# A list scheduler with refitted durations and an attention rank 100 places ahead, in a three-branch mixer kernel

## Chip, cores and metric

One core of one Trainium2 chip runs the whole program. The metric is the device time of one launch in microseconds (us), the median of several runs. The engines are PE (matrix products, transposes), ACT, DVE and POOL (elementwise work), and SP, whose queue issues the DMAs.

## What is computed

Two layers over 512 latent tokens and a prefix of 256 context tokens, width 1024, all fp32. Cut to what matters:

```python
for l in range(2):
    h  = rms_norm(x, g_pre) * (1 + scale) + shift          # also for the context tokens
    rk, rv, dk, dv, rq, rg, dq, dg, mu, mv, mg, mlog = split(h @ w_in[l])
    # (A) retention, 4 heads, chunks of 128, both directions, rotary q and k
    ret  = rms_norm(bidir_retention(rope(rq), rope(rk), rv)) * silu(rg)
    # (B) gated MLP with 128x128 position mixing
    mlp  = mu * (w_s @ layer_norm(mv) + b_s) * silu(mg)
    # (C) differential attention, 4 heads, keys = context + latent (768)
    p    = softmax(q @ k.T / 8)                             # two maps per head
    dif  = rms_norm((p[0] - lam * p[1]) @ dv) * silu(dg)
    y    = sum(sigmoid(logit_b) * (branch_b @ w_bo[b]) for the three branches)
    x    = x + gate * rms_norm(y @ w_out[l], g_post)
```

In the second layer the context tokens only give keys, values and a final retention state.

## The kernel before

**Products.** A large product is made of three fp32r products of high and low parts (`xs`, `ws`): activations and weights are split into a rounded high part (copied by ACT) and the rest (a subtraction on DVE). Weights come in blocks of 2048 or 1536 words per partition, by one DMA each into one of two raw buffers, and are split into one of two slots (`w_split`, 512 words at a time). A projection takes a tile of PSUM in the first two of eight banks; ACT or DVE empties it (`.ev`), and only then can the tile after next be written.

**Attention unit** (`d_unit`, one head and 128 queries, 32 of them with six key tiles, 8 with two): PE makes the scores of two maps in three banks that all units share; DVE takes the maxima (L370); ACT makes two exponentials with sums (L339); DVE combines them (L378, L360, L366); PE transposes the result (L318); ACT copies it; PE multiplies by the values (L314, fp32, two records per instruction in the profile); then a norm over ACT, DVE and POOL, one transpose and a copy. **Retention unit** (`r_state`, `r_attn`): similar, shorter chains.

**Order of the code.** `dr_phase` walks through the projections of the attention and retention branches in the order of `ORDER`; after each tile `step` lets one or two finished units be recorded (`pop`), so the units lie between projections whose results they don't need. After it come the gates (`dg`), merges, the MLP and the output. Each `add` records one operation with its engine, a cost in ns, what it reads and writes, and a rank: its place in the recording, plus `bump`:

```python
o.prio = o.i + self.bump
```

Weight splits are recorded with a bump of -20 (`WBUMP`), so they rank 20 places ahead.

**Scheduler.** `Rec.schedule` plays the recorded operations against its own costs: an engine that is free takes the lowest rank among the operations that are ready, an operation is ready when all that it depends on have ended plus `LATENCY[from, to]`. What comes out is one fixed order per engine, and the instructions are emitted in it. On the chip each engine works through its own queue in that order and waits on semaphores: an operation that is not ready holds up all behind it, ready or not.

Of the kernel before, what the change touches and what calls it, by code (L numbers as in the profile page):

```python
# [12 lines left out]
ALU = mybir.AluOpType  # L13
AX = mybir.AxisListType
# [172 lines left out]
class Op:  # L187
# [1 line left out]

LATENCY = {("PE", "ACT"): 200, ("PE", "DVE"): 200, ("PE", "SP"): 200, ("ACT", "PE"): 290, ("ACT", "DVE"): 100, ("ACT", "POOL"): 100,
           ("ACT", "SP"): 100, ("ACT", "ACT"): 100, ("DVE", "PE"): 290, ("DVE", "ACT"): 150, ("DVE", "POOL"): 170, ("DVE", "DVE"): 127,
           ("DVE", "SP"): 100, ("POOL", "PE"): 150, ("POOL", "ACT"): 65, ("POOL", "DVE"): 65, ("POOL", "POOL"): 102, ("POOL", "SP"): 100}

WINDOW = 3413.3

# [1 line left out]
class Rec:  # L199
# [123 lines left out]
    def act(self, out, in_, func, bias=None, scale=1.0, accum=None):  # L323
        kw = {}
        ins, outs = [in_], [out]
        if bias is not None:
            kw["bias"] = bias
            if not isinstance(bias, float):
                ins.append(bias)
        if not isinstance(scale, float):  # L330
            ins.append(scale)
        kw["scale"] = scale
        c = self.n(in_) / 1.19 + (160 if self.ps(in_) else 195) + 198 * (accum is not None) + 60 * (len(ins) - 1)
        if accum is not None:
            kw["accum_out"] = accum
            outs.append(accum)
        tab = "e" if func == AF.Exp else "s" if func == AF.Sigmoid else None
        e = self.nc.scalar
        return self.add("ACT", lambda: e.activation(out, in_, func, **kw), outs, ins, c, tab)  # L339
# [3 lines left out]

    def copy_v(self, out, in_):
        v = self.nc.vector
        c = self.n(in_) / (0.96 if self.ps(in_) or self.ps(out) else 1.92) + 160
        return self.add("DVE", lambda: v.tensor_copy(out, in_), [out], [in_], c)

    def tt(self, out, a, b, op):
        v = self.nc.vector  # L350
        return self.add("DVE", lambda: v.tensor_tensor(out, a, b, op=op), [out], [a, b], self.n(out) / 0.97 + 168)  # L351

    def ts(self, out, a, s1, s2=None, op0=ALU.mult, op1=None):
        v = self.nc.vector
        ins = [a] + [s for s in (s1, s2) if s is not None and not isinstance(s, float)]
        c = self.n(out) * (1.04 if self.ps(a) else 0.52) + 160 + 60 * (len(ins) - 1)
        if op1 is None:
            f = lambda: v.tensor_scalar(out, a, s1, None, op0=op0)  # L358
        else:
            f = lambda: v.tensor_scalar(out, a, s1, s2, op0=op0, op1=op1)  # L360
        return self.add("DVE", f, [out], ins, c)

    def stt(self, out, a, s, b, op0, op1):
        v = self.nc.vector
        ins = [a, b] + ([] if isinstance(s, float) else [s])
        return self.add("DVE", lambda: v.scalar_tensor_tensor(out, a, s, b, op0=op0, op1=op1), [out], ins, self.n(out) / 0.97 + 215)  # L366

    def red(self, out, in_, op):
        v = self.nc.vector
        return self.add("DVE", lambda: v.tensor_reduce(out, in_, axis=AX.X, op=op), [out], [in_], self.n(in_) / 0.96 + 155)  # L370

    def ttr(self, junk, a, b, accum):
        v = self.nc.vector
        return self.add("DVE", lambda: v.tensor_tensor_reduce(junk, a, b, 1.0, 0.0, ALU.mult, ALU.add, accum), [junk, accum], [a, b], self.n(a) / 0.96 + 290)  # L374

    def recip(self, out, in_):
        v = self.nc.vector
        return self.add("DVE", lambda: v.reciprocal(out, in_), [out], [in_], self.n(in_) * 6.25 + 155)  # L378

    def bn_stats(self, out, in_):  # L380
        v = self.nc.vector
        return self.add("DVE", lambda: v.bn_stats(out, in_), [out], [in_], self.n(in_) / 0.96 + 155)

    def bn_aggr(self, out, in_):
        v = self.nc.vector
        return self.add("DVE", lambda: v.bn_aggr(out, in_), [out], [in_], 172)

    def ptt(self, out, a, b, op):
        g = self.nc.gpsimd
        n = self.n(out)  # L390
        c = 600 + 150 * n if op == ALU.pow else 2.4 * n + 250
        return self.add("POOL", lambda: g.tensor_tensor(out, a, b, op=op), [out], [a, b], c)  # L392

    def memset(self, out, val):
# [9 lines left out]
    def schedule(self):  # L404
# [23 lines left out]
        while ev:  # L428
# [4 lines left out]
            while again:  # L433
                again = False
                for e in self.ENG:
# [13 lines left out]

                    t0 = max((x + LATENCY[f, e] for b in o.banks for f, x in held[b].items() if (f == "PE") != (e == "PE")), default=0.0)  # L450
                    if t0 > t:
# [26 lines left out]
                    for s in succ[i]:  # L478
                        left[s] -= 1
                        at[s] = max(at[s], o.done + LATENCY.get((e, ops[s].eng), 0))  # L480
                        if left[s] == 0:
# [78 lines left out]
NBUF = 4  # L560
BUMP = 400
WBUMP = -20
H_LO = 6144
RING = (12288, 16384)
Z = 20480
# [5 lines left out]
class Prog:  # L571
    def __init__(self, nc, R, AR, AFl, PSM, ap):
# [4 lines left out]
        self.HH = self.arv(0, 8, NT)  # L577
        self.HL = self.arv(H_LO, 8, NT)
        self.raws = {}
# [61 lines left out]
    def w_split(self, i):  # L641
# [9 lines left out]
        step = 512  # L651
        R.bump = WBUMP
        for a in range(0, w, step):
# [67 lines left out]
    def pop(self):  # L721
        f = (self.side[0] or self.side[1]).pop(0)[1]
        t = self.R.tag
        f()
        self.R.tag = t

    def until(self, key):
# [1137 lines left out]
```

## Time and profile before

| | |
|---|---|
| median of 3 runs | 1536.49 us (1535.66 to 1537.17) |
| the profiled execution | 1536.63 us |
| its span, first to last instruction | 1534.9 us |
| PE busy | 1505.0 us, 98% |
| PE weight loads busy | 1350.8 us, 88% |
| DVE / ACT / POOL busy | 799.0 / 602.3 / 168.9 us |
| TensorE clock granted | 1.00 of full, from the start to the end |
| DMA | 156.32 MB, mean 102 GB/s |

The profiled execution lies 1.7 us above its span and 0.14 us above the median. A row of the timeline merges instructions of one kind that follow each other; the time in square brackets is the idle time of the engine before the row, with the instruction that ended it. The end of a matrix product is modelled and lies after the time at which the next product may start, so of a row of n products the array is taken for less than its length.

### The profile page before, as it was taken

The page shows a single profiled execution, that of the slowest core. Times are in us where ns is not written, and L with a number is a line of the kernel's source. Part 1 is how long each engine was busy: PE and PEld are TensorE (multiplying, and loading weights), DVE is VectorE, ACT ScalarE, POOL GpSimd, SP SyncE. Part 2 cuts the span into 40 slices and gives each one's busy share as a digit, 9 for nine tenths or more (in the row PEclk, how much of TensorE's full clock was granted, in tenths as well). Part 3 has the DMA queues.
Part 4 walks back from the last instruction along what each step waited for, and adds up shares of the span by engine and source line. Part 5 has one row for each costly group of instructions (what it writes and reads, how often), then busy time and mean ns, then how long its engine had stood idle before and what let it go on. Part 6 is the DMA issues. An engine that isn't in the chain of part 4 may idle for free.

```text
span 1534.9 us, 23633 instructions
## 1 busy us (share of the span) xinstructions
PE 1505.0 (98%) x9544; PEld 1350.8 (88%) x9544; DVE 799.0 (52%) x1551; ACT 602.3 (39%) x1298; POOL 168.9 (11%) x187
## 2 busy tenths in 40 slices
PE   7999999999999999999999999999999999999998
PEld 4799998989888888989889999989988888898888
DVE  4457635655333872235874654674656434344452
ACT  6735543573222222222223463464455333332341
POOL 1212201110000011001000131111110000201000
PEclk9999999999999999999999999999999999999999
DMA  9441312111231442122563223241211332321331
GB/s 364 144 138 56 86 40 76 50 52 63 75 116 54 165 138 83 56 74 88 187 201 124 97 101 121 86 117 49 83 42 56 103 117 83 118 98 65 119 124 69
DMA packets 37710, 156.32 MB, mean 102 GB/s; under 512 B 5345, under 2 KB 6497, under 8 KB 31201
## 3 DMA queue, kind: packets, MB, share of 16 engines
q1 hardware_dynamic: 37600, 154.81, 30.0%
q8 instruction: 75, 1.23, 0.3%
q14 instruction: 35, 0.28, 0.1%
HBM read 132.77 MB, written 4.19 MB: 89 GB/s over the span
## 4 chain that ended last, share of the span: by engine, by line
PE 94%; issue 1%; DVE 1%; ACT 1%; DMA 0%; POOL 0%; SPq 0%; DVEq 0%; POOLq 0%; ACTq 0%
PE PSM L314 91%; PE PSM L318 3%; ACT AF L339 1%; DMA AF<-AF 0%; POOL AF L392 0%; DVE AR L351 0%; SPq L401 0%; DVE AF L351 0%; DVE AF L366 0%; DVE AF L370 0%; ACT AR L339 0%; DVE AF L360 0%; DVE AF L378 0%; DVEq L1861 0%; POOLq L1861 0%
## 5 line engine op out<-in xcount | busy, mean ns | idle before, releaser
L314 PE MATMUL PSM<-AR 128*128 128x256 f32 (+1 forms) x8016 | 1361.8, 330 | 9.1 <-ACT AF L339 7.3
L314 PEld LDWEIGHTS PSM<-AR 128*128 128x128 f32 x8016 | 1186.5, 190 | 140.7 <-ACT AF L339 9.6
L339 ACT ACTIVATE AR<-AF 128x512 fp32r<-128x512 f32 (+4 forms) x489 | 285.2, 607 | 422.3 <-PE PSM L314 295.9
L351 DVE TENSOR_TENSOR AR<-AF,AR 128x512 fp32r<-128x512 f32 (+4 forms) x486 | 318.6, 673 | 252.6 <-ACT AR L339 205.2
L339 ACT ACTIVATE AF<-PSM 128x512 f32<-128x512 f32 (+4 forms) x385 | 170.5, 462 | 392.1 <-PE PSM L314 324.3
L392 POOL TENSOR_TENSOR AF<-AF 128x1 f32<-128x1 f32 (+5 forms) x180 | 168.2, 943 | 1360.9 <-DVE AF L360 588.5
L351 DVE TENSOR_TENSOR AF<-PSM,AF 128x512 f32<-128x512 f32 (+2 forms) x253 | 144.7, 581 | 236.6 <-PE PSM L314 111.8
L314 PE MATMUL PSM<-AF 128*128 128x128 f32 (+3 forms) x1104 | 143.9, 304 | 12.4 <-DMA AF<-wmodn 8.9
L314 PEld LDWEIGHTS PSM<-AF 128*128 128x128 f32 (+1 forms) x1104 | 127.2, 184 | 23.9 <-DVE AF L360 9.3
L339 ACT ACTIVATE AF<-PSM,AF 128x768 f32<-128x768 f32 (+2 forms) x144 | 91.9, 648 | 64.9 <-DVE AF L358 40.5
L374 DVE CUSTOM_DVE_ANT_0 AR<-AF 128x1024 fp32r<-128x1024 f32 x59 | 76.5, 1296 | 14.8 <-DMA AF<-wmod 8.8
L370 DVE TENSOR_REDUCE AF<-PSM 128x2 f32<-128x1536 f32 (+1 forms) x40 | 61.4, 1541 | 35.7 <-PE PSM L314 35.6
L360 DVE TENSOR_SCALAR AF<-AF 128x1 f32<-128x1 f32 (+3 forms) x188 | 42.5, 237 | 61.5 <-ACT AF L339 58.3
L318 PE MATMUL PSM<-AF 128*128 128x128 f32 x424 | 67.5, 277 | 2.1 <-DVE AF L366 1.2
L339 ACT ACTIVATE AF<-AF 128x256 f32<-128x256 f32 (+4 forms) x107 | 54.7, 558 | 20.4 <-POOL AF L392 10.3
L318 PEld LDWEIGHTS PSM<-AF 128*128 128x128 f32 x424 | 51.2, 142 | 13.1 <-ACT AF L339 3.2
L351 DVE TENSOR_TENSOR AF<-AF 128x512 f32<-128x512 f32 (+5 forms) x78 | 42.9, 555 | 13.2 <-PE PSM L318 5.0
L366 DVE SCALAR_TENSOR_TENSOR AF<-AF 128x768 f32<-128x768 f32 (+2 forms) x48 | 43.5, 913 | 3.6 <-POOL AF L392 2.7
L366 DVE SCALAR_TENSOR_TENSOR AF<-AF,PSM 128x128 f32<-128x128 f32 x64 | 19.8, 344 | 20.5 <-PE PSM L314 12.0
L358 DVE TENSOR_SCALAR AF<-AF 128x2 f32<-128x2 f32 (+4 forms) x98 | 20.4, 223 | 7.0 <-PE PSM L314 3.4
L360 DVE TENSOR_SCALAR AF<-PSM,AF 128x128 f32<-128x128 f32 x48 | 15.9, 404 | 12.0 <-PE PSM L318 11.9
L351 DVE TENSOR_TENSOR AR<-PSM,AR 64x256 fp32r<-64x256 f32 x24 | 10.1, 421 | 21.2 <-ACT AR L339 21.0
(20 smaller groups left out, 94.3 us busy)
## 6 DMA issues: line engine op xcount, KB each, us to landing
AF<-w SPq DMA_DIRECT2D x50, 1024.0 KB, 4.8
AF<-w SPq DMA_DIRECT2D x48, 768.0 KB, 4.2
AF<-wmod SPq DMA_DIRECT2D x32, 512.0 KB, 3.6
AF<-wmodn SPq DMA_DIRECT2D x16, 512.0 KB, 8.9
AF<-x SPq DMA_DIRECT2D x12, 512.0 KB, 4.2
AR<-AR SPq DMA_DIRECT2D x16, 384.0 KB, 4.6
AF<-AF SPq DMA_DIRECT2D x64, 64.0 KB, 2.3
AR<-AF SPq DMA_DIRECT2D x12, 256.0 KB, 2.3
```

The source lines that it names most:

```text
L314: self.add("PE", lambda: pe.matmul(out, lhsT, rhs, start=start, stop=stop), [out], [lhsT, rhs], c)
L318: self.add("PE", lambda: pe.transpose(out, in_, ident), [out], [in_, ident], 109.0)
L339: return self.add("ACT", lambda: e.activation(out, in_, func, **kw), outs, ins, c, tab)
L351: return self.add("DVE", lambda: v.tensor_tensor(out, a, b, op=op), [out], [a, b], self.n(out) / 0.97 + 168)
L358: f = lambda: v.tensor_scalar(out, a, s1, None, op0=op0)
L360: f = lambda: v.tensor_scalar(out, a, s1, s2, op0=op0, op1=op1)
L366: return self.add("DVE", lambda: v.scalar_tensor_tensor(out, a, s, b, op0=op0, op1=op1), [out], ins, self.n(out) / 0.97 + 215)
L370: return self.add("DVE", lambda: v.tensor_reduce(out, in_, axis=AX.X, op=op), [out], [in_], self.n(in_) / 0.96 + 155)
L374: return self.add("DVE", lambda: v.tensor_tensor_reduce(junk, a, b, 1.0, 0.0, ALU.mult, ALU.add, accum), [junk, accum], [a, b], self.n(a) ...
L392: return self.add("POOL", lambda: g.tensor_tensor(out, a, b, op=op), [out], [a, b], c)
```

## The change

The latencies between engines and the fixed parts of the costs on ACT, DVE and POOL get new numbers, nearly all smaller; costs on PE and of DMAs stay. Whatever `pop` records (attention and retention units, with the code that ends a head) gets a bump of -100. No operation is added or removed, and what depends on what stays: only the orders differ.

```diff
-LATENCY = {... ("ACT", "PE"): 290, ("ACT", "DVE"): 100, ("ACT", "POOL"): 100,
-           ("ACT", "SP"): 100, ("ACT", "ACT"): 100, ("DVE", "PE"): 290, ("DVE", "ACT"): 150, ("DVE", "POOL"): 170, ("DVE", "DVE"): 127,
-           ("DVE", "SP"): 100, ("POOL", "PE"): 150, ("POOL", "ACT"): 65, ("POOL", "DVE"): 65, ...}
+LATENCY = {... ("ACT", "PE"): 153, ("ACT", "DVE"): 133, ("ACT", "POOL"): 177,
+           ("ACT", "SP"): 135, ("ACT", "ACT"): 135, ("DVE", "PE"): 137, ("DVE", "ACT"): 119, ("DVE", "POOL"): 163, ("DVE", "DVE"): 117,
+           ("DVE", "SP"): 117, ("POOL", "PE"): 93, ("POOL", "ACT"): 73, ("POOL", "DVE"): 73, ...}
 # act
-        c = self.n(in_) / 1.19 + (160 if self.ps(in_) else 195) + 198 * (accum is not None) + 60 * (len(ins) - 1)
+        c = self.n(in_) / 1.19 + (60 if self.ps(in_) else 95) + 150 * (accum is not None) + 88 * (len(ins) - 1)
 # tt (copy_v, ts, red, recip, bn_stats, bn_aggr in the same way, some 84 less; stt 85 less, ttr 140 less)
-        return self.add("DVE", lambda: v.tensor_tensor(out, a, b, op=op), [out], [a, b], self.n(out) / 0.97 + 168)
+        return self.add("DVE", lambda: v.tensor_tensor(out, a, b, op=op), [out], [a, b], self.n(out) / 0.97 + 84)
 # ptt
-        c = 600 + 150 * n if op == ALU.pow else 2.4 * n + 250
+        c = 560 + 150 * n if op == ALU.pow else 2.4 * n + 210
...
+ABUMP = -100
...
     def pop(self):
         f = (self.side[0] or self.side[1]).pop(0)[1]
         t = self.R.tag
+        self.R.bump = ABUMP
         f()
+        self.R.bump = 0
         self.R.tag = t
```

The orders themselves, at three places of PE's queue. `PSM<-AR` are fp32r products: in these places x2 of 512 columns and x2 or x4 of 256 are the scores of an attention unit, x24 of 256 is half of a projection's pair of tiles, x12 of 512 half of a tile. `L318` are transposes, `L314 ... PSM<-AF 128x128 x6` the products of one unit with its values.

**Place A**, PE, layer 0, units 1 and 2 of the last attention head. Before (the first, second, fifth and sixth rows are the scores of unit 1; the last two begin those of unit 2):

```order
L314 MATMUL PSM<-AR 128x512 x2
L314 MATMUL PSM<-AR 128x256 x2
L318 MATMUL PSM<-AF 128x128
L314 MATMUL PSM<-AF 128x128 x2
L314 MATMUL PSM<-AR 128x256 x2
L314 MATMUL PSM<-AR 128x512 x2
L318 MATMUL PSM<-AF 128x128 x8
L314 MATMUL PSM<-AR 128x512 x2
L314 MATMUL PSM<-AR 128x256 x2
```

After (scores of unit 1 in the first three rows, scores of unit 2 from the last row on):

```order
L314 MATMUL PSM<-AR 128x512 x2
L314 MATMUL PSM<-AR 128x256 x4
L314 MATMUL PSM<-AR 128x512 x2
L314 MATMUL PSM<-AR 128x256 x24
L318 MATMUL PSM<-AF 128x128
L314 MATMUL PSM<-AF 128x128 x6
L314 MATMUL PSM<-AR 128x256 x24
L318 MATMUL PSM<-AF 128x128 x7
L314 MATMUL PSM<-AR 128x512 x2
```

Between the two units' scores stood eight transposes; now a whole pair of projection tiles, six products and eight transposes stand there.

**Place B**, PE, layer 0, the last query projection of retention (`rq1`, x12 of 512) and the key-value projection after it (`rkv3`, x24 of 256). Before:

```order
L314 MATMUL PSM<-AR 128x512 x16
L314 MATMUL PSM<-AR 128x256 x2
L314 MATMUL PSM<-AR 128x512 x12
L314 MATMUL PSM<-AR 128x256 x24
L314 MATMUL PSM<-AR 128x512 x2
```

After (the first row ends `rq1`; the third is another tile pair of `rkv3`, whose PSUM was emptied long before; the pair that needs the tile of `rq1` is the end of the last row):

```order
L314 MATMUL PSM<-AR 128x512 x14
L314 MATMUL PSM<-AF 128x128 x6
L314 MATMUL PSM<-AR 128x256 x24
L318 MATMUL PSM<-AF 128x128 x7
L314 MATMUL PSM<-AR 128x512 x2
L314 MATMUL PSM<-AR 128x256 x4
L314 MATMUL PSM<-AR 128x512 x2
L314 MATMUL PSM<-AF 128x128 x6
L314 MATMUL PSM<-AR 128x256 x24
L318 MATMUL PSM<-AF 128x128
L314 MATMUL PSM<-AR 128x256 x32
```

The tile that is written next after `rq1` was the one that `rq1` itself had just filled before; now two halves of another pair and two units' work come between.

**Place C**, PE, layer 1, units 0 to 2 of the last attention head. Before (the first two rows end the scores of unit 1, the sixth, seventh, ninth and tenth are those of unit 2, the eleventh transposes unit 1 and the twelfth multiplies it):

```order
L314 MATMUL PSM<-AR 128x256 x2
L314 MATMUL PSM<-AR 128x512 x2
L318 MATMUL PSM<-AF 128x128 x2
L314 MATMUL PSM<-AF 128x128 x6
L318 MATMUL PSM<-AF 128x128 x2
L314 MATMUL PSM<-AR 128x512 x2
L314 MATMUL PSM<-AR 128x256 x2
L318 MATMUL PSM<-AF 128x128
L314 MATMUL PSM<-AR 128x256 x2
L314 MATMUL PSM<-AR 128x512 x2
L318 MATMUL PSM<-AF 128x128 x6
L314 MATMUL PSM<-AF 128x128 x6
```

After (the first row ends the scores of unit 1; the seventh transposes unit 1, the last multiplies it):

```order
L314 MATMUL PSM<-AR 128x512 x2
L318 MATMUL PSM<-AF 128x128 x8
L314 MATMUL PSM<-AR 128x256 x24
L318 MATMUL PSM<-AF 128x128
L314 MATMUL PSM<-AF 128x128 x6
L314 MATMUL PSM<-AR 128x256 x24
L318 MATMUL PSM<-AF 128x128 x7
L314 MATMUL PSM<-AR 128x512 x2
L314 MATMUL PSM<-AR 128x256 x4
L314 MATMUL PSM<-AR 128x512 x2
L314 MATMUL PSM<-AF 128x128 x6
```

Two halves of a projection pair now stand between the scores of unit 1 and its transposes, where before stood only small work of the units themselves, and the next unit's scores stand between the transposes and the product.

Elsewhere: PE's order is the same from the second layer's first merge to the end; from the first layer's first merge to that layer's end only a few neighbours change places. On SP the first 59 DMA issues stand as before, and none of the 318 moves by more than 5 places. On ACT and DVE an operation moves by 2 to 3 places in the mean, at most by some 30.

## Rows read from the trace of the kernel before

**Rows 1.** The page's part 1: PE's busy time, share of the span, instructions.
```profile
PE 1505.0 (98%) x9544; PEld 1350.8 (88%) x9544; DVE 799.0 (52%) x1551; ACT 602.3 (39%) x1298; POOL 168.9 (11%) x187
```

**Rows 2.** Stretches: length, busy time of each engine, clock, DMA share, GB/s.
```profile
8.90:24.00 15.10, 13.01 (x69) 5.94 (x70) 8.05 (x23) 9.82 (x18) 3.94 (x6) 1.00 1.04 405
24.00:62.00 38.00, 38.00 (x252) 28.69 (x253) 20.77 (x84) 27.88 (x72) 0.46 (x1) 1.00 0.62 230
62.00:398.00 336.00, 328.70 (x2268) 303.26 (x2267) 189.49 (x392) 165.39 (x419) 54.35 (x71) 1.00 0.23 72
398.00:913.00 515.00, 515.00 (x3317) 471.12 (x3316) 272.61 (x503) 157.86 (x289) 44.64 (x37) 1.00 0.34 116
913.00:1201.00 288.00, 282.62 (x1905) 258.00 (x1904) 169.62 (x314) 134.30 (x303) 41.73 (x48) 1.00 0.25 77
1201.00:1517.20 316.20, 316.20 (x1646) 272.50 (x1646) 131.26 (x219) 102.13 (x188) 21.57 (x15) 1.00 0.29 103
```

**Rows 3.** PE's waits, 62 to 400 us: releaser, us in total, times, longest.
```profile
PE PSM L314 <- ACT AF L339: 5.1, 4, 2.5
PE PSM L314 <- DVE AF L351: 1.6, 1, 1.6
PE PSM L318 <- ACT AF L339: 0.5, 1, 0.5
```

**Rows 4.** PE's waits, 1000 to 1200 us.
```profile
PE PSM L314 <- ACT AF L339: 4.0, 4, 1.1
PE PSM L318 <- DVE AF L366: 1.2, 3, 0.5
```

**Rows 5.** Timeline at place A: start, us, engine, instruction, count, idle before.
```profile
308.30 1.04 PE L318 MATMUL PSM<-AF 128*128 128x128 f32 x8
308.50 1.76 DVE L370 TENSOR_REDUCE AF<-PSM 128x2 f32<-128x1536 f32 x1 [1.52 <-PE PSM L314]
311.85 0.97 PE L314 MATMUL PSM<-AR 128*128 128x512 f32 x4 [2.51 <-ACT AF L339]
312.65 0.27 PE L318 MATMUL PSM<-AF 128*128 128x128 f32 x1
312.76 1.50 PE L314 MATMUL PSM<-AF 128*128 128x128 f32 x12
```

**Rows 6.** Timeline at place B, PE.
```profile
266.94 2.30 PE L314 MATMUL PSM<-AR 128*128 128x256 f32 x17 [1.64 <-DVE AF L351]
```

**Rows 7.** Timeline at place C.
```profile
1136.38 1.76 DVE L370 TENSOR_REDUCE AF<-PSM 128x2 f32<-128x1536 f32 x1 [1.74 <-PE PSM L314]
1139.48 1.39 PE L314 MATMUL PSM<-AR 128*128 128x512 f32 x4 [1.12 <-ACT AF L339]
1142.00 0.87 PE L318 MATMUL PSM<-AF 128*128 128x128 f32 x6 [0.31 <-DVE AF L366]
1142.91 0.81 ACT L339 ACTIVATE AF<-PSM 128x768 f32<-128x768 f32 x1 [1.61 <-PE PSM L318]
1143.77 1.60 PE L314 MATMUL PSM<-AF 128*128 128x128 f32 x12 [0.90 <-ACT AF L339]
```

**Rows 8.** Timeline, layer 1, second head, unit 2: its reduction and its transposes.
```profile
1024.38 1.76 DVE L370 TENSOR_REDUCE AF<-PSM 128x2 f32<-128x1536 f32 x1
1032.18 0.87 PE L318 MATMUL PSM<-AF 128*128 128x128 f32 x6 [0.48 <-DVE AF L366]
```

**Rows 9.** Back-to-back products: the chain that ended last (start, us), then the timeline.
```profile
857.27 2.88 PE PSM L314 x24
```
```profile
1390.69 5.70 PE L314 MATMUL PSM<-AR 128*128 128x512 f32 x24
```

**Rows 10.** Timeline: three equal instructions in a row on ACT, and on DVE.
```profile
296.04 1.68 ACT L339 ACTIVATE AR<-AF 128x512 fp32r<-128x512 f32 x3
296.84 1.89 DVE L351 TENSOR_TENSOR AR<-AF,AR 128x512 fp32r<-128x512 f32 x3
```

**Rows 11.** Timeline of the start, ACT: one 256-wide weight split.
```profile
10.46 0.42 ACT L339 ACTIVATE AR<-AF 128x256 fp32r<-128x256 f32 x1 [3.93 <-DMA AF<-w]
```

More of the change, by code (lines that the diff above doesn't have):

```diff
@@ L188 @@
     pass
-LATENCY = {("PE", "ACT"): 200, ("PE", "DVE"): 200, ("PE", "SP"): 200, ("ACT", "PE"): 290, ("ACT", "DVE"): 100, ("ACT", "POOL"): 100,
-           ("ACT", "SP"): 100, ("ACT", "ACT"): 100, ("DVE", "PE"): 290, ("DVE", "ACT"): 150, ("DVE", "POOL"): 170, ("DVE", "DVE"): 127,
-           ("DVE", "SP"): 100, ("POOL", "PE"): 150, ("POOL", "ACT"): 65, ("POOL", "DVE"): 65, ("POOL", "POOL"): 102, ("POOL", "SP"): 100}
+LATENCY = {("PE", "ACT"): 200, ("PE", "DVE"): 200, ("PE", "SP"): 200, ("ACT", "PE"): 153, ("ACT", "DVE"): 133, ("ACT", "POOL"): 177,
+           ("ACT", "SP"): 135, ("ACT", "ACT"): 135, ("DVE", "PE"): 137, ("DVE", "ACT"): 119, ("DVE", "POOL"): 163, ("DVE", "DVE"): 117,
+           ("DVE", "SP"): 117, ("POOL", "PE"): 93, ("POOL", "ACT"): 73, ("POOL", "DVE"): 73, ("POOL", "POOL"): 102, ("POOL", "SP"): 100}
 WINDOW = 3413.3
@@ L345, in copy_v @@
         v = self.nc.vector
-        c = self.n(in_) / (0.96 if self.ps(in_) or self.ps(out) else 1.92) + 160
+        c = self.n(in_) / (0.96 if self.ps(in_) or self.ps(out) else 1.92) + 76
         return self.add("DVE", lambda: v.tensor_copy(out, in_), [out], [in_], c)
@@ L355, in ts @@
         ins = [a] + [s for s in (s1, s2) if s is not None and not isinstance(s, float)]
-        c = self.n(out) * (1.04 if self.ps(a) else 0.52) + 160 + 60 * (len(ins) - 1)
+        c = self.n(out) * (1.04 if self.ps(a) else 0.52) + 76 + 60 * (len(ins) - 1)
         if op1 is None:
@@ L365, in stt @@
         ins = [a, b] + ([] if isinstance(s, float) else [s])
-        return self.add("DVE", lambda: v.scalar_tensor_tensor(out, a, s, b, op0=op0, op1=op1), [out], ins, self.n(out) / 0.97 + 215)
+        return self.add("DVE", lambda: v.scalar_tensor_tensor(out, a, s, b, op0=op0, op1=op1), [out], ins, self.n(out) / 0.97 + 130)
     def red(self, out, in_, op):
         v = self.nc.vector
-        return self.add("DVE", lambda: v.tensor_reduce(out, in_, axis=AX.X, op=op), [out], [in_], self.n(in_) / 0.96 + 155)
+        return self.add("DVE", lambda: v.tensor_reduce(out, in_, axis=AX.X, op=op), [out], [in_], self.n(in_) / 0.96 + 72)
     def ttr(self, junk, a, b, accum):
         v = self.nc.vector
-        return self.add("DVE", lambda: v.tensor_tensor_reduce(junk, a, b, 1.0, 0.0, ALU.mult, ALU.add, accum), [junk, accum], [a, b], self.n(a) / 0.96 + 290)
+        return self.add("DVE", lambda: v.tensor_tensor_reduce(junk, a, b, 1.0, 0.0, ALU.mult, ALU.add, accum), [junk, accum], [a, b], self.n(a) / 0.96 + 150)
     def recip(self, out, in_):
         v = self.nc.vector
-        return self.add("DVE", lambda: v.reciprocal(out, in_), [out], [in_], self.n(in_) * 6.25 + 155)
+        return self.add("DVE", lambda: v.reciprocal(out, in_), [out], [in_], self.n(in_) * 6.25 + 72)
     def bn_stats(self, out, in_):
         v = self.nc.vector
-        return self.add("DVE", lambda: v.bn_stats(out, in_), [out], [in_], self.n(in_) / 0.96 + 155)
+        return self.add("DVE", lambda: v.bn_stats(out, in_), [out], [in_], self.n(in_) / 0.96 + 72)
     def bn_aggr(self, out, in_):
         v = self.nc.vector
-        return self.add("DVE", lambda: v.bn_aggr(out, in_), [out], [in_], 172)
+        return self.add("DVE", lambda: v.bn_aggr(out, in_), [out], [in_], 88)
     def ptt(self, out, a, b, op):
```

## Prediction

> **What bounds the kernel now.** I read the page first: PE is busy for 1505.0 of 1534.9 us [rows 1]. Then the stretches, since that share is an average: in three of them PE is busy all the time, 38.00 of 38.00, 515.00 of 515.00 and 316.20 of 316.20 us [rows 2]; there no order can win anything, and only a new gap can lose. PE is idle in the two stretches in which attention and retention run: 336.00 - 328.70 = 7.3 us in layer 0 and 288.00 - 282.62 = 5.4 us in layer 1. The clock is 1.00 in all of them. Third, PE's waits there: 4 + 1 + 1 waits with 7.2 us [rows 3], 4 + 3 waits with 5.2 us [rows 4]; ACT or DVE ends every one, no DMA does. So 13 waits hold 12.4 us. A wait costs a little more than its idle time, since the last product before it runs out: a transpose alone lasts 0.27 us [rows 5], while eight in a row last 1.04, so followers come every (1.04 - 0.27) / 7 = 0.11 us; the difference is 0.16 us a wait, 2.1 us for 13. **Together 14.5 us**, 0.9% of the time, is what a better order could save here. The rest is the start, before 24 us, and the closing work after the last product.
>
> Fourth, the timeline at the waits, to see whether the order makes them. Place A: unit 1's scores are followed by eight transposes (0.88 us) and then by unit 2's scores, which overwrite the banks that unit 1's exponential still reads. The reduction begins at 308.50, the scores can go on at 311.85, 3.35 us later, of which PE idles 2.51 [rows 5]. Place B: a projection stands right behind the one whose PSUM it needs emptied: 1.64 us [rows 6]. Place C: from unit 1's reduction to its transposes 1142.00 - 1136.38 = 5.62 us pass, and PE has 3.3 us of products to put there; 1.12, 0.31 and 0.90 us of idle follow [rows 7]. These orders put too little between a result and the product that needs it.
>
> **The numbers that the scheduler gets.** Are the new ones nearer to the trace? Three equal ACT copies take 1.68 us and three DVE subtractions 1.89 [rows 10]. The new costs for 512 columns are 512 / 1.19 + 95 = 525 ns and 512 / 0.97 + 84 = 612, three of them 1.58 and 1.84 us; the old ones, 625 and 696 ns, make 1.88 and 2.09. At place C the copy starts at 1142.91 and the product that waits for it at 1143.77, 0.86 us later [rows 7]; new: 768 / 1.19 + 60 = 705 ns and 153 of latency, 0.86; old: 805 + 290, 1.10. So the old table placed a waiting product about a quarter of a microsecond late per hop, and an engine free about 0.1 us late; the new one is right within 0.1.
>
> **The change, term by term.**
>
> *The 13 waits, -14.5 us.* I count the products between result and user in the new order, with 0.12 us for 256 columns (2.88 / 24) and 0.23 for 512 (5.70 / 24) [rows 9], 0.11 for a transpose and 1.34 for a unit's six value products (twelve records in 1.50 us, the first 0.27 [rows 5]). Place A: 24 x 0.12 + 0.11 + 1.34 + 24 x 0.12 + 0.77 = 8.0 us where 3.35 are needed. Place B: 11.7 us in place of none. Place C: 0.88 + 2.88 + 0.11 + 1.34 + 2.88 = 8.1 us in place of 3.3, where 5.8 are needed (5.62 and about 0.2 from the last score to the reduction, as from the transposes' end on the array, 1142.71, to the copy at 1142.91). Between the transposes and the product stand 1.39 us of scores and a transpose, in place of nothing: 1.5. In the same way for the 32 units with six key tiles, scores to transposes: before, the shortest counts were 3.28, 3.39, 5.83, 6.00 and 6.44 us; in the new order 5.90, 5.94, 5.94, 6.16, 6.45, 6.45, 6.79, 6.84, 6.90, 6.90, four of 7.06, 7.09, three of 7.10, three of 7.21, 7.32, 7.38, 7.47, 7.49, 7.60, 7.76 and five above. None lies under the 5.8 us of place C. So all 13 go.
>
> *New waits, +3.2 us.* Tighter numbers leave no slack for queues: ACT and DVE serve units, tiles and weight splits in one fixed order, and a unit that meets others takes longer. The slowest row is a unit of layer 1: 1032.18 - 1024.38 = 7.80 us, with the 0.2 us 8.0 [rows 8]. I take 6.5 us, nearer to place C than to this one, since the new table knows the queues and place C's row is what an unhindered unit takes: the counts under 6.5 fall short by 0.60 + 0.56 + 0.56 + 0.34 + 0.05 + 0.05 = 2.2 us. One mean wait of before (12.4 / 13 = 1.0 us) comes on top for evictions, retention and splits that now stand behind units. Bounds: 0, and 5.7 us at a need of 7.0.
>
> *Rank -100.* By itself it moves work of ACT and DVE, both half idle there (ACT 165.39 and DVE 189.49 of 336.00 us [rows 2]). What it pushes back, evictions and weight splits, hides behind the counts above: a tile's PSUM is needed again at the earliest 2.3 us after a projection that fills it, in place of 0.
>
> *DMA, 0.* Issues move by at most 5 places on SP; the DMA engines are busy 0.23 of the stretch [rows 2] and no wait of PE ends with one. Without that cover a weight block that comes late would stop PE, which no row of these stretches shows.
>
> *The start, 0.* From 24 us on PE has no gap, before it 15.10 - 13.01 = 2.1 us [rows 2]. The order changes by a few places on ACT: an input tile's scaling goes ahead of a split that waited 3.93 us for its DMA, later two splits of 0.42 us go ahead of copies PE needs [rows 11]. Between -2.1 and +0.8 us.
>
> *The end, 0:* the same order on PE, and no idle time to win.
>
> **Sum:** -14.5 + 3.2 = -11.3 us against the profiled 1536.63, that is 1525.3; the median of the runs stands 0.14 lower, so **1525.2 us**.
>
> **How full PE is.** The rows above take PE's busy time at its word. In the stretch without idle time the weight loads are busy 471.12 / 515.00 = 91.5%; in the two with waits 90.3 and 89.6% [rows 2]. If 91.5% is full, the room is (0.915 x 336.00 - 303.26) + (0.915 x 288.00 - 258.00) = 4.2 + 5.5 = 9.7 us, less than the 14.5 above; the mix of shapes differs, so I keep 14.5. The Trainium skill (Perfetto Trace Analysis, Identifying the Most-Contended Engine) says that matmul busy time misleads and that headroom is to be judged by the share of the weight loads; taken alone, with 1350.8 of 1534.9 us, that would leave 184 us. The trace speaks against so much: a stretch without any gap stays at 91.5%.
>
> **The rivals.**
>
> *Half of it comes back.* Chains take 7.2 us or so, and the shortfall is 8 to 11 us: 1530 to 1533.4. For it: 18 of the 32 counts lie between 5.9 and 7.2 us, so one steady delay hits many at once. Against: at 7.2 the old counts would fall short by 12 us in this place alone, of 14.5 in all, and places A and B took their part of these elsewhere.
>
> *Slower: the units' chains run as long as the slowest row.* Place: scores to transposes, all 32 units. If each takes 8.0 us, the new counts fall short by 28.5 us; less 14.5 that is +14.0, 1550.6. It decides from a mean need of about 7.5 us on, where the shortfall reaches 14.5. For it: exactly that row exists, and units that rank ahead of everything meet each other. Against: the old counts at 8.0 would have cost over 19.5 us, and the waits were 14.5 in all.
>
> *No change.* The idle time only moves: what PE gains at the waits it loses at the first merges, because ACT and DVE have the same work to finish. 1533.5 to 1539.6. Against: ACT and DVE are about half busy in these stretches.
>
> *More than that.* All 14.5 us, the start's 2.1, and products that run denser than busy time shows: under 1520.
>
> **How the numbers follow.** My forecast (1520 to 1530) has a chance of 0.72, half of it back 0.13, no change 0.08, slower 0.05, more 0.02. The range reaches from all waits and the start's gap gone, 1536.6 - 14.5 - 2.1 = 1520, to the end of the half-back case: 1520 to 1533. A measurement of this kernel can tell 0.2%, 3.1 us, from no change; so faster (under 1533.4) 0.87, same 0.08, slower 0.05.
>
> **What would show it.** Right: in the new profile PE's waits between 62 and 400 and between 1000 and 1200 us sum to 2 to 5 us, the row before unit 1's transposes in place C has no idle bracket, PE's busy time falls little while the span loses 11 us, and the stretches from the first merges on stay without a gap. Wrong: new brackets of 0.3 to 1 us at many transposes behind a DVE combination (half back, or slower), or brackets with weight splits or a DMA as the releaser. The prediction is wrong if the span stays above 1531.7 us.

## The result and the profile after

The changed kernel takes **1523.53 us** (median of 4 runs, 1523.48 to 1524.99); the kernel before, beside it, 1536.83 us (1535.66 to 1538.02). The ratio is 0.9916, 95% interval 0.9899 to 0.9933. The forecast was 1525.2 us in a range of 1520 to 1533. The profiled execution takes 1523.52 us with a span of 1521.7, against 1534.9: 13.2 us less.

The page's first part, after, for [rows 1]:

```profile
PE 1500.7 (99%) x9544; PEld 1350.5 (89%) x9544; DVE 794.2 (52%) x1551; ACT 600.0 (39%) x1298; POOL 167.8 (11%) x187
```

The stretches of the new profile, with boundaries at the same work as in [rows 2]:

```profile
8.90:24.00 15.10, 11.61 (x68) 5.82 (x69) 8.36 (x25) 9.85 (x19) 4.09 (x5) 1.00 1.04 404
24.00:62.00 38.00, 38.00 (x256) 28.60 (x253) 20.95 (x83) 27.82 (x75) 1.33 (x3) 1.00 0.61 232
62.00:391.00 329.00, 326.62 (x2265) 301.88 (x2264) 188.97 (x391) 163.66 (x417) 54.82 (x69) 1.00 0.24 74
391.00:903.00 512.00, 512.00 (x3278) 467.54 (x3278) 270.76 (x503) 155.51 (x286) 43.68 (x37) 1.00 0.34 114
903.00:1188.00 285.00, 285.00 (x1947) 263.06 (x1946) 166.36 (x314) 136.40 (x306) 39.02 (x48) 1.00 0.27 82
1188.00:1504.00 316.00, 316.00 (x1646) 272.37 (x1645) 131.43 (x219) 101.82 (x188) 21.47 (x15) 1.00 0.30 102
```

The attention stretch of layer 0 has 2.4 us of idle PE left (7.3 before), that of layer 1 none (5.4 before). PE's waits after, 62 to 400 us, for [rows 3]; between 900 and 1200 us ([rows 4]) this view has no row:

```profile
PE PSM L318 <- ACT AF L339: 1.7, 3, 1.0
PE PSM L314 <- DVE AF L351: 0.6, 1, 0.6
```

**Where the 13.2 us come from.** Compare when the same product, the one in the same place of PE's order, begins in both traces. At 24 us the difference is nothing, at the end of layer 0's attention phase it is 5.2 us (403.14 before, 397.95 after), it stays there through the merges and the MLP, and in layer 1 it grows to 13.2 us at the last head (1156.37 and 1143.21) and remains so to the end. Layer 0 gave 5.2 us, layer 1 gave 8.0. PE's idle time of 5.2 us [rows 4] doesn't explain 8.0 in layer 1. The row that does is the one of PE's weight loads: a wait shorter than the tail of the product before it leaves no gap between products, but the weight load behind it starts late. Waits of the weight loads before, first 62 to 400 us, then 900 to 1200 us:

```profile
PEld PSM L314 <- ACT AF L339: 6.0, 4, 2.7
PEld PSM L314 <- DVE AF L351: 2.1, 1, 2.1
PEld PSM L318 <- ACT AF L339: 0.7, 1, 0.7
PEld PSM L318 <- DVE AF L366: 0.3, 1, 0.3
```
```profile
PEld PSM L314 <- ACT AF L339: 6.1, 7, 1.4
PEld PSM L318 <- DVE AF L366: 2.4, 3, 0.8
PEld PSM L318 <- ACT AF L339: 0.7, 2, 0.5
```

and after:

```profile
PEld PSM L318 <- ACT AF L339: 2.8, 3, 1.5
PEld PSM L314 <- DVE AF L351: 0.8, 1, 0.8
PEld PSM L314 <- DVE AR L351: 0.3, 1, 0.3
PEld PSM L314 <- ACT AF L339: 0.3, 1, 0.3
PEld PSM L318 <- DVE AF L351: 0.2, 1, 0.2
```
```profile
PEld PSM L318 <- DVE AF L366: 0.4, 1, 0.4
```

In layer 1 before, these are 9.2 us in 12 waits, where PE's own row shows 5.2 us in 7. Over both stretches the weight loads wait 18.3 us before and 4.8 after. The difference, 13.5, is the 13.2 us of the span within 0.3; by layers it is 4.7 against 5.2 and 8.8 against 8.0, so it holds within 0.8. Below I call this sum "late loads".

**Place C** now, PE's timeline (scores of unit 1 in the first row, its transposes in the seventh, the scores of the next unit in the eighth, unit 1's value products in the last):

```profile
1114.38 1.64 PE L314 MATMUL PSM<-AR 128*128 128x512 f32 x8
1115.86 1.03 PE L318 MATMUL PSM<-AF 128*128 128x128 f32 x8
1116.65 3.11 PE L314 MATMUL PSM<-AR 128*128 128x256 f32 x24
1119.60 0.27 PE L318 MATMUL PSM<-AF 128*128 128x128 f32 x1
1119.71 1.50 PE L314 MATMUL PSM<-AF 128*128 128x128 f32 x12
1120.97 3.12 PE L314 MATMUL PSM<-AR 128*128 128x256 f32 x24
1123.92 0.93 PE L318 MATMUL PSM<-AF 128*128 128x128 f32 x7
1124.61 1.65 PE L314 MATMUL PSM<-AR 128*128 128x512 f32 x8
1126.09 1.50 PE L314 MATMUL PSM<-AF 128*128 128x128 f32 x12
```

No row has an idle bracket, where three stood [rows 7]. From the end of the scores to the transposes 8.1 us of products pass, as counted.

**The new wait.** The longest stands in layer 0, where a unit's normalised result is transposed. The timeline there:

```profile
255.91 2.53 POOL L392 TENSOR_TENSOR AF<-AF 128x512 f32<-128x512 f32 x2 [11.14 <-DVE AF L378]
...
256.23 1.80 DVE L366 SCALAR_TENSOR_TENSOR AF<-AF 128x768 f32<-128x768 f32 x1
...
258.47 0.37 ACT L339 ACTIVATE AF<-PSM,AF 128x128 f32<-128x128 f32 x1 [2.26 <-POOL AF L392]
...
258.90 0.98 PE L318 MATMUL PSM<-AF 128*128 128x128 f32 x7 [1.03 <-ACT AF L339]
```

The x2 of the first row merges two operations; by form they are:

```profile
L392 POOL TENSOR_TENSOR AF<-AF 128x512 f32<-128x512 f32 x1 | 1.3, 1297 | 11.1 <-DVE AF L378 11.1
L392 POOL TENSOR_TENSOR AF<-AF 128x1 f32<-128x1 f32 x1 | 1.3, 1274 | 0.0
```

The unit's power for its norm (128x1) stood behind a rotary product on POOL and then took 1274 ns itself, where the scheduler counts 560 + 150 = 710. The trace shows what held it. Of the 62 powers of this size, the 36 that run while DVE does nothing take 0.55 to 0.56 us. The seven that begin 0.16 us or more after a 128x768 combination on DVE (L366) has begun all end 0.41 to 0.42 us after that combination, and so take 1.25 to 1.27 us. Here the combination, 1.00 us by itself at 986.32, took 1.80 beside the rotary product, and the power, begun at 257.17, ended 0.42 us behind it.

The other two ACT-ended waits, at 138.64 and 268.43, end at the same kind of transpose. The one at 268.43 stands behind one of these seven powers (1263 ns). At 138.64 the power was done in time (0.55 us from 137.31 on), and ACT first ran an exponential of the next unit.

### The profile page after: what moved, and what is told of

Its sections match the earlier page's. It is cut to its first block, busy times and chain, and to the rows that moved or that the text cites. A ratio compares the mean times of both kernels' runs of the same rounds, so it can differ in the third digit from the quotient of the medians.

```text
span 1521.7 us, 23656 instructions
## 1 busy us (share of the span) xinstructions
PE 1500.7 (99%) x9544; PEld 1350.5 (89%) x9544; DVE 794.2 (52%) x1551; ACT 600.0 (39%) x1298; POOL 167.8 (11%) x187
## 4 chain that ended last, share of the span: by engine, by line
PE 94%; DVE 2%; issue 1%; ACT 1%; POOL 0%; DMA 0%; SPq 0%; DVEq 0%; POOLq 0%; ACTq 0%
PE PSM L314 91%; PE PSM L318 3%; DVE AR L351 1%; POOL AF L392 0%; ACT AF L339 0%; DVE AF L351 0%; DVE AF L370 0%; DMA AF<-AF 0%; SPq L401 0%; DVE AF L366 0%; ACT AR L339 0%; DVE AF L360 0%; DVEq L1864 0%; POOLq L1864 0%; DVE AF L358 0%
## 5 line engine op out<-in xcount | busy, mean ns | idle before, releaser
L314 PE MATMUL PSM<-AR 128*128 128x256 f32 (+1 forms) x8016 | 1361.5, 330 | 0.7 <-DVE AF L351 0.6
L314 PEld LDWEIGHTS PSM<-AR 128*128 128x128 f32 x8016 | 1186.6, 190 | 130.6 <-issue 1.2
L351 DVE TENSOR_TENSOR AR<-AF,AR 128x512 fp32r<-128x512 f32 (+3 forms) x486 | 315.6, 666 | 280.0 <-ACT AR L339 232.6
L392 POOL TENSOR_TENSOR AF<-AF 128x128 f32<-128x128 f32 (+5 forms) x180 | 167.1, 937 | 1348.9 <-DVE AF L351 513.8
L339 ACT ACTIVATE AF<-PSM 128x256 f32<-128x256 f32 (+4 forms) x385 | 170.1, 462 | 352.1 <-PE PSM L314 319.0
L314 PE MATMUL PSM<-AF 128*128 128x128 f32 (+3 forms) x1104 | 141.7, 300 | 11.4 <-DMA AF<-wmodn 9.1
L314 PEld LDWEIGHTS PSM<-AF 128*128 128x128 f32 (+1 forms) x1104 | 126.9, 184 | 21.7 <-DVE AF L374 9.0
L318 PE MATMUL PSM<-AF 128*128 128x128 f32 x424 | 67.6, 276 | 2.7 <-ACT AF L339 2.7
L318 PEld LDWEIGHTS PSM<-AF 128*128 128x128 f32 x424 | 50.9, 141 | 12.5 <-ACT AF L339 4.8
L366 DVE SCALAR_TENSOR_TENSOR AF<-AF 128x768 f32<-128x768 f32 (+2 forms) x48 | 43.1, 905 | 3.8 <-POOL AF L392 2.7
L366 DVE SCALAR_TENSOR_TENSOR AF<-AF,PSM 128x128 f32<-128x128 f32 x64 | 19.9, 344 | 11.7 <-ACT AF L339 5.8
L339 ACT ACTIVATE AR<-PSM 64x256 fp32r<-64x256 f32 x24 | 9.1, 378 | 27.4 <-PE PSM L314 27.1
```

What stands on the lines that cost most here:

```text
L314: self.add("PE", lambda: pe.matmul(out, lhsT, rhs, start=start, stop=stop), [out], [lhsT, rhs], c)
L318: self.add("PE", lambda: pe.transpose(out, in_, ident), [out], [in_, ident], 109.0)
```

## Experiments

Each kernel was timed with the kernel before on the same chip (medians of 1536.68 to 1537.08 us there), and the ratio is to that. The table sets all of them side by side; "late loads" is the sum over 62 to 400 and 900 to 1200 us of its profiled execution. The dot marks what is as before.

| run | costs | latencies | rank | us, median (range) | ratio to before (95%) | late loads, us |
|---|---|---|---|---|---|---|
| before | . | . | . | 1536.83 (1535.66 to 1538.02) | 1 | 18.3 |
| the change | new | new | -100 | 1523.53 (1523.48 to 1524.99) | 0.9916 (0.9899 to 0.9933) | 4.8 |
| table_only | new | new | . | 1528.73 (1527.46 to 1531.14) | 0.9945 (0.9933 to 0.9957) | 10.8 |
| rank_only | . | . | -100 | 1538.65 (1537.44 to 1540.68) | 1.0012 (1.0003 to 1.0020) | 17.9 |
| costs_only | new | . | . | 1525.38 (1524.26 to 1526.04) | 0.9922 (0.9909 to 0.9935) | 6.4 |
| lat_only | . | new | . | 1538.38 (1534.08 to 1540.11) | 1.0003 (0.9995 to 1.0012) | 16.7 |
| occupancy_only | new | chains as before | . | 1523.60 (1522.63 to 1524.13) | 0.9916 (0.9902 to 0.9930) | 4.1 |
| costs_rank | new | . | -100 | 1529.14 (1528.74 to 1529.98) | 0.9954 (0.9941 to 0.9966) | 9.9 |
| rank_back | new | new | +100 | 1599.80 (1597.37 to 1601.01) | 1.0415 (1.0399 to 1.0431) | 53.5 |
| lat_low | new | new x 0.3 | -100 | 1544.42 (1541.99 to 1546.21) | 1.0053 (1.0040 to 1.0065) | 25.9 |
| dve_costs | DVE, POOL new | . | . | 1527.40 (1526.83 to 1527.61) | 0.9938 (0.9926 to 0.9951) | 8.4 |
| act_costs | ACT new | . | . | 1527.92 (1527.20 to 1528.64) | 0.9942 (0.9929 to 0.9954) | 8.9 |
| rank_minus_50 | new | new | -50 | 1524.27 (1522.58 to 1525.53) | 0.9920 (0.9907 to 0.9934) | 4.5 |
| occ_rank | new | chains as before | -100 | 1531.30 (1530.80 to 1532.64) | 0.9965 (0.9953 to 0.9978) | 10.4 |

Nine of these traces keep the full clock until the closing work (all but rank_only, lat_only, rank_back, lat_low and occ_rank). In these the profiled span less the late loads is 1516.1 to 1517.9 us, while the spans reach from 1520.8 to 1534.9: what sets the orders apart is their late loads.

**The two halves: table_only and rank_only.**

```diff
 # table_only, against the change      # rank_only, against before
-ABUMP = -100                          +self.R.bump = ABUMP   (-100, in pop)
+ABUMP = 0
```

> All new costs and latencies, rank bump 0. Theory TABLE (the order is better because the scheduler knows how long a chain takes): nearly the whole gain stays, 1524 to 1528 us, since in this order one six-tile unit alone has a short count from scores to transposes (3.39 us, 2.4 short of 5.8), the next ones 6.16 and more. Theory RANK (units ahead of projections make it): 1533 to 1538 us.

> Old costs and latencies, rank bump -100. Theory TABLE: no gain, 1534 to 1539 us, since the shortest six-tile counts stay 2.84, 3.39 and 5.83 us (5.4 short of 5.8 in all, 4.9 in the kernel before). Theory RANK: 1523 to 1528 us.

The table gives 8.4 us without the rank, the rank without the table loses 1.6 (its late loads are no more than before; its clock falls, last section). Together they give 13.3, so the rank adds about 5 on the new table: no sum of two parts.

**The two halves of the table: costs_only and lat_only.**

```diff
 # costs_only: the old LATENCY in the change, ABUMP = 0
 # lat_only: only the new LATENCY in the kernel before
```

> New costs on ACT, DVE and POOL, old latencies, rank bump 0. If the engines' occupancy is what the old table had wrong: 1525 to 1529 us (counts: one of 3.39 us, the next 6.16). If the latencies to PE are: 1533 to 1537 us.

> Old costs, new latencies, rank bump 0. If the costs matter most: 1532 to 1537 us (one six-tile count of 3.28 us, then 5.83, 5.89; projections still stand right behind tiles that they need emptied). If the latencies do: 1525 to 1529 us.

The costs alone give 11.7 us; by its interval, 0.9922 (0.9909 to 0.9935), this isn't told apart from the whole change. The latencies alone give nothing in the median, and 1.6 us of late loads. "Nearly all smaller" holds for the costs. Of the 13 latencies that change, only six are smaller, all three to PE among them (290 to 153, 290 to 137, 150 to 93), and seven are larger. So of the table it is the costs on ACT, DVE and POOL that count, not the time from an engine's end to the reader's start. Whether they count through the queues or through the chains, the next run asks.

**Chain or queue: occupancy_only.** A lower cost shortens both the time for which the engine is taken and the chain through it. Here the first is new and the second stays: what the costs lose is added to the latency behind them (an exponential with its sum, which lost 48 ns more and gained 28, stays 20 ns short).

```diff
-LATENCY = {... ("ACT", "PE"): 290, ("ACT", "DVE"): 100, ... ("DVE", "PE"): 290, ("DVE", "DVE"): 127, ... ("POOL", "PE"): 150, ...}
+LATENCY = {... ("ACT", "PE"): 390, ("ACT", "DVE"): 200, ... ("DVE", "PE"): 374, ("DVE", "DVE"): 211, ... ("POOL", "PE"): 190, ...}
 # with the new costs, ABUMP = 0
```

> New costs, and old latencies raised by what the costs lost (ACT 100, DVE 84, POOL 40 ns), rank bump 0: the scheduler sees chains as long as before, but engines that come free sooner. Theory QUEUE (the old table overstated how long ACT and DVE are taken, so what waits behind other work was placed too late): 1524 to 1529 us, as with the new costs alone. Theory CHAIN (it overstated how long a chain takes): 1533 to 1539 us.

1523.60 us, the time of the whole change, without the rank and with chains counted as long as before. Its PE waits, 62 to 400 us:

```profile
PE PSM L314 <- ACT AF L339: 0.5, 1, 0.5
```

**The rank on other tables: costs_rank, rank_back, rank_minus_50, occ_rank.**

```diff
 # costs_rank: the change with the old LATENCY
 # rank_back: the change with ABUMP = 100; rank_minus_50: with ABUMP = -50
 # occ_rank: occupancy_only with ABUMP = -100
```

> New costs, old latencies, rank bump -100. If the rank's gain adds to that of the costs: 1520 to 1524 us. If the rank gains only with the new latencies: 1526 to 1534 us, since in this order two six-tile units have short counts, 2.84 and 3.39 us, 5.4 short of 5.8 in all.

> New costs and latencies, rank bump +100 in place of -100: units come after the projections. Theory FILL (projections are the work that fills PE between two steps of a unit, and whoever uses them up first leaves the last units bare): the counts of the six-tile units fall short of 5.8 us by 23.8 us in all, the chains of the last units stand with nothing between, 1555 to 1580 us. If only the table matters: 1524 to 1530 us.

> The whole change with a rank of -50 in place of -100. COUNTS theory (what is left of waits is what the counts fall short of 6.5 us): they fall short by 0.9 us in place of 2.2, so 1521.5 to 1523 us. PLACE theory (which unit meets which projection at a given rank is chance; rank moves the time by some us with either sign and no count says which): 1524 to 1529. The rank theory by which a smaller head start gives back a part of the gain: about 1526, half-way to the new table without the rank (1528.7).

> New costs with old chain lengths (latencies raised by what the costs lost) and the rank of -100. Without the rank this table gave 1523.6 us. If the rank helps for itself, as it did with the new latencies (-5.2): 1518 to 1521. PLACE theory (its sign depends on the table, as with the new costs and the old latencies, where it lost 3.8): 1525 to 1531. By the counts, which fall short of 6.5 us by 8.0 in place of 4.0: about 1527.5.

The rank of -100 gains about 5 us on the new table, loses 3.8 on the new costs with the old latencies (1529.14 and 1525.38) and 7.7 on occupancy_only (1531.30 and 1523.60). A rank of -50 measures the same as -100. The sign thus belongs to the pair of table and rank. Putting the units 100 places behind the projections costs 71 us against the same table with rank 0 (1599.80 and 1528.73), 63 against the kernel before. That the last units are left bare, as theory FILL has it, fits the direction, but its range ended at 1580 and I have not traced it further. PE's waits of rank_back, 62 to 400 us:

```profile
PE PSM L314 <- ACT AF L339: 11.5, 11, 2.7
PE PSM L314 <- DVE AF L351: 5.3, 4, 2.7
PE PSM L318 <- ACT AF L339: 1.2, 3, 0.5
PE PSM L318 <- DVE AF L366: 0.9, 1, 0.9
```

Late loads explain 50 of its 61 us of span (53.5, and 15.0 in stretches that had none, less 18.3). The rest fits the falls of the clock (last section), which I had not in the expectation.

**Latencies too low: lat_low.**

```diff
-LATENCY = {("PE", "ACT"): 200, ... ("ACT", "PE"): 153, ("ACT", "DVE"): 133, ...}
+LATENCY = {("PE", "ACT"): 60, ... ("ACT", "PE"): 45, ("ACT", "DVE"): 39, ...}
```

> As the changed kernel, but all latencies times 0.3. Theory TIGHT (a scheduler that thinks results come too soon puts their users too early and PE waits): nine of the six-tile counts lie between 5.3 and 5.8 us, short of 6.2 by 5.1 us in all, so 1526 to 1533 us. If small errors of the table cost nothing: 1522 to 1525 us.

21 us more than the change, and more than I expected: an order that counts on every result too early waits a little at many places, 40 late loads in place of 8. Latencies of a third of the new ones hurt, while those up to 0.24 us above the new ones (occupancy_only) didn't.

**Which engine's costs: dve_costs and act_costs.**

```diff
 # dve_costs: before, with the change's costs in copy_v, tt, ts, stt, red, ttr, recip, bn_stats, bn_aggr, ptt
 # act_costs: before, with the change's cost in act
```

> Only the costs on DVE and POOL are new; ACT's costs, the latencies and the rank are the old ones. The costs of all three engines together gave -11.7 us against the kernel before. DVE theory (what counts is how long the scheduler thinks DVE occupied, since a unit's long reductions and combinations run there and DVE is the busier of the two): 1526 to 1529 us, most of the gain. SUM theory (each engine's costs are worth a part, since a unit's chain crosses both): 1529 to 1533. ACT theory (ACT's 100 ns a copy were the error that counted): 1534 to 1538. The scores-to-transposes counts of the six-tile units keep the two shortest ones of before, 3.28 and 3.39 us, so they fall short of 6.5 us by 6.3 (before 7.6): by counts alone about 1535.

> The complement: only ACT's costs are new. DVE theory 1534 to 1538 us; SUM theory 1529 to 1533; ACT theory 1525 to 1529. The counts fall short of 6.5 us by 8.4 (before 7.6): by counts alone about 1537.

Either half alone gives about 9 us, both 11.7. Each half lies in the range of the theory that put the gain in that half alone, so neither of these theories holds, nor the one by which the shares add up. The counts failed as well: act_costs falls short of 6.5 us at its scores by 8.4 us, before by 7.6, and yet 9 of its 18 us of late loads are gone. The count of products between scores and transposes, on which my forecast leaned, doesn't by itself tell one table from another.

No run beat the change by more than its interval; occupancy_only and rank_minus_50 measure the same. The medians of table_only, lat_only, occupancy_only and occ_rank lie up to 1.4 us outside the range of the theory that they speak for, those of rank_back and lat_low 20 and 11 us above it.

One rival is left untested: that the old order was a poor draw, and that most changes of the costs would have given a better one. For it: the nine orders with new costs, in whole or in half, with latencies not below the new ones and units not behind projections, spread from 1523.5 to 1531.3 us. Against it: the two other orders made with old costs are no faster than the old one, and all nine are. No run changed the costs away from what the trace shows.

## Why the prediction was right, and where it wasn't

- **What bounds it: right.** The gain lies in the two attention stretches, the gapless ones stayed gapless, DMA and the end gave nothing. PE's waits sum to 2.3 us, within the 2 to 5 named as a sign. PE's busy time falls by 4.3 us, a third of what the span loses: "falls little" is right in part, since busy time holds waits that hide in it (next point). At the start PE is 13.01 - 11.61 = 1.4 us less busy between 8.90 and 24.00 us, yet at 24 us the same product begins at the same time in both (24.23 and 24.20): 0, as forecast.
- **"So all 13 go": right, and undersized.** The waits of places A, B and C are gone (a new one of 0.20 us, at 268.43, stands at the transposes in the fourth row of place B after). But "the last product before it runs out, 0.16 us a wait" counted only the waits that PE's own row shows. The late loads before are 18.3 us, not 14.5; layer 0 is near the forecast (9.1, against 7.2 + 6 x 0.16 = 8.2), layer 1 is not (9.2, against 5.2 + 7 x 0.16 = 6.3). There the seven waits that PE's row shows measure 7.3 us at the weight loads, 0.3 us more each and not 0.16, and five more, 1.9 us, hide under the tail of the product before.
- **"New waits, +3.2": size nearly right, place wrong.** There are 4.8 us of late loads after. The six counts below 6.5 us, for which 2.2 us were set, made none of the waits that PE's row shows: none of its four ends at a score chain, three end at the transpose of a normalised result and one at a projection (97.69). The term reasoned with queues on ACT and DVE. One of the three is that; two hang on POOL, which the term doesn't name. So 6.5 us was too much for the scores, and one mean wait of 1.0 us too little for all the rest. The two misses of the sum, 18.3 - 14.5 = 3.8 us too little gained and 4.8 - 3.2 = 1.6 too little lost, partly cancel, and to that extent the closeness is luck; the result lies 1.7 us below the forecast.
- **"Rank -100 by itself nothing": right alone, wrong in company.** On the old table the time moves by +0.12% (0.03 to 0.20), with 17.9 us of late loads in place of 18.3. On the new table it is worth some 5 of the 13 us, which the forecast put down to the table.
- **"The old table placed a waiting product a quarter of a microsecond late per hop": right as a reading of the hops into PE, wrong as the reason.** Correcting latencies alone does nothing, and the gain comes whole with chains left long. "An engine free about 0.1 us late", half a sentence in the forecast, is the part of the change that the runs show to bring the gain. How that plays out product by product I have not traced through; that an order for a busier ACT and DVE spaces their work wrongly is an argument only.
- **How full PE is.** The room from the weight loads' share, 9.7 us, was too small: after the change the two stretches stand at 301.88 / 329.00 = 91.8% and 263.06 / 285.00 = 92.3%. The Trainium skill (Perfetto Trace Analysis, Identifying the Most-Contended Engine) advises to judge headroom by that share, and by the share of peak work, in place of the products' busy time. The trace agrees that the products' time misleads: PE's row doesn't give the 13.2 us. But the share itself has no fixed ceiling here. In stretches of the new kernel in which PE is busy throughout it is 263.06 / 285.00 = 92%, 467.54 / 512.00 = 91%, 272.37 / 316.00 = 86% and 28.60 / 38.00 = 75%. What is missing to 100% is no room by itself, and the 91.5% of the forecast holds for its own mix of products alone. What did give the 13.2 us are the waits in the weight loads' row.
- **The rivals.** Half back, slower and no change didn't come. The slower one wanted chains of 8.0 us at all units; after counts from 5.90 us up, PE's row shows no wait at a score chain (the one late load of 0.4 us in layer 1, at 987.37, ends at one).

## What to carry to other kernels

When a list scheduler orders the work, fit how long each engine is taken (from rows of several equal instructions in a row, not from one alone) before the latencies; leave latencies rather too high than too low, as far as one kernel can tell. Treat a rank or bias as a thing to try again with each table, since its sign changed with the table here. For room that better order can win, read the waits of the weight loads, not of the products, and look at the end of each unit as closely as at its start: a short operation on POOL can take twice its time beside one on DVE, and a cost per operation doesn't know that.

## What was unexpected of the hardware

**TensorE's clock falls to half behind some short waits, and not behind others like them.** The kernel before and lat_only have the same cluster of waits at unit 2 of layer 1's second head. PE's timeline before:

```profile
1030.62 0.97 PE L314 MATMUL PSM<-AR 128*128 128x256 f32 x4 [1.08 <-ACT AF L339]
1031.43 0.27 PE L318 MATMUL PSM<-AF 128*128 128x128 f32 x1
1032.18 0.87 PE L318 MATMUL PSM<-AF 128*128 128x128 f32 x6 [0.48 <-DVE AF L366]
1033.95 1.60 PE L314 MATMUL PSM<-AF 128*128 128x128 f32 x12 [0.90 <-ACT AF L339]
```

and of lat_only:

```profile
1031.22 0.97 PE L314 MATMUL PSM<-AR 128*128 128x256 f32 x4 [1.11 <-ACT AF L339]
1032.03 0.27 PE L318 MATMUL PSM<-AF 128*128 128x128 f32 x1
1032.79 1.41 PE L318 MATMUL PSM<-AF 128*128 128x128 f32 x6 [0.48 <-DVE AF L366]
1035.09 2.93 PE L314 MATMUL PSM<-AF 128*128 128x128 f32 x12 [0.90 <-ACT AF L339]
```

The idle times are equal within 0.03 us, but the twelve products take 2.93 us in place of 1.60. In lat_only's stretches the granted clock (the third number from the end) falls from full to half, 1.2 GHz, at 1033 us. Two of the waits, 1.11 and 0.48 us, lie before the fall, the third after it. The clock is back at 1040 us; PE has worked without a gap from 1035.09 on:

```profile
1032.00:1033.00 1.00, 0.52 (x4) 0.22 (x3) 1.00 (x2) 0.28 (x1) 0.00 (x0) 0.99 0.82 186
1033.00:1034.00 1.00, 1.00 (x6) 0.79 (x4) 1.00 (x1) 0.00 (x0) 0.00 (x0) 0.50 0.98 410
...
1038.00:1039.00 1.00, 1.00 (x7) 1.00 (x6) 0.21 (x1) 0.95 (x3) 0.25 (x1) 0.50 0.57 131
1039.00:1040.00 1.00, 1.00 (x7) 1.00 (x6) 0.59 (x3) 0.67 (x3) 0.29 (x1) 0.60 0.58 131
1040.00:1041.00 1.00, 1.00 (x11) 1.00 (x10) 0.86 (x1) 0.00 (x0) 0.74 (x1) 1.00 0.00 0
```

From the four 256-wide products to the end of the next 48 lat_only takes 2.6 us more than before. Such falls stand in the traces of lat_only, rank_only, occ_rank, lat_low and rank_back; in rank_back there are several, and the clock is 0.97 in the mean from 62 to 400 us. Place A is a second pair: behind 2.51 us of idle the kernel before keeps the full clock and its twelve products take 1.50 us [rows 5], behind 2.57 us at the same place rank_only falls to half and they take 2.56. The runs of one kernel spread with it: the span of lat_only is 1532.3 us in the two runs with a mean clock of 0.999 and 1537.5 to 1538.2 in the three with 0.996 (the seven between have 1534.3 to 1538.3). So a wait can cost more than its length; which one does, nothing here foretells. A few tenths of a per cent between two orders with waits say little. Before and after, as profiled, fall only in the last 2 to 4 us of the closing work (so the clock of 1.00 "from the start to the end" holds up to there), and the 13.2 us are waits alone. The Trainium skill (TensorE: Matmul & The Clock Gate, HAM oscillation — how this bites in real kernels) tells of the clock falling again and again at long waits on DMA between groups of products; in lat_only waits of 1.11 and 0.48 us behind ACT and DVE stood before a fall.
